# A two-layer encoder on one core: the 64-row score products become 128-row products with a zero-padded q

## The chip, the core and the metric

The kernel runs on one core of a Trainium2 chip. A core has five engines that work side by side, each through its own list of instructions in order: TensorE (PE in the profile; its weight loads are shown apart as PEld), VectorE (DVE), ScalarE (ACT), GpSimd (POOL) and SyncE (SP), which here issues all the DMA transfers. They wait for each other by semaphores. The metric is the device time of one execution in microseconds (us); less is better.

## What is computed

The reference is an encoder with 512 tokens of width 1024 and two layers. Each layer has a token mixer, a cross-attention into 256 memory tokens and a feed-forward part, each between two norms with a residual. Layer 1's mixer is dilated attention with 16 heads of 64 (layer "a"), layer 2's is differential attention with 8 pairs of heads of 64 (layer "b"). All in float32.

```python
def reference(x, mem, positions, ...):
    h = x
    for i in range(DEPTH):
        u = rms_norm(h, mix_pre_g[i])
        if kind == 0:
            y = dilated_attention_mixer(u, a_w_in[j], a_w_out[j], cos, sin)
        elif kind == 1:
            y = differential_attention_mixer(u, b_w_in[j], b_w_out[j], ..., cos, sin, i)
        ...
        h = h + rms_norm(y, mix_post_g[i])
        u = rms_norm(h, mem_pre_g[i])
        y = memory_cross_attention(u, rms_norm(mem, mem_kv_g[i]), x_wq[i], x_wkv[i], x_wo[i])
        h = h + rms_norm(y, mem_post_g[i])
        u = rms_norm(h, ffn_pre_g[i])
        y = swiglu_ffn(u, w_gate_up[i], w_down[i])
        h = h + rms_norm(y, ffn_post_g[i])
    return h
```

Both mixers need, for each head, scores q·k over 64 features for 512 queries by 512 keys, with q and k turned by a rotary embedding first.

## The kernel before

**Precision.** Every float32 operand of a matrix product is split into a high part (type fp32r in the profile) and a low part (what the high part left over). A product is then three products of parts: high·high, high·low and low·high. The splits cost one pass of ScalarE (high) and one of VectorE or GpSimd (low). For weights these are lines 237 and 238, after a DMA of 512 KB into one of two staging buffers `raw` (line 221).

**Scores.** A head has 64 features, so two of the three products fit into one: the stack `st[e]` of q holds q's high part of head e in 64 rows and its low part in the other 64, and k's stack holds k's high part twice. Line 645 multiplies the two over 128 rows, which gives high·high + low·high. Line 646 adds q high · k low over the 64 rows `a` of that head; k's low part `kl` holds both heads of a pair, one above the other. Each such pair of products fills one bank of PSUM (128 queries x 512 keys). A mixer has 8 pairs of heads (p = 0..7), each with 2 heads (e) and 4 blocks of 128 queries (qb): 64 score pairs in each layer, 128 in all.

**Making the stacks.** After the product that gives q of a pair, `q_stack` (line 577) applies the rotary embedding (`rope`: lines 560 and 561 on VectorE, 562 and 563 on GpSimd), makes the high part on ScalarE (line 592) and the low part on VectorE (line 594). Since the low part of a head belongs in the other 64 rows, `half_copies` (line 570) moves the four halves by DMA on SP's queue (line 573), 128 KB each. `k_stack` (line 600) does the same for k. Pair 7 (`DIRECT`) is written by the engines straight into the stacks (lines 586 and 587), without copies. The stacks of pairs p and p+2 share their memory.

**Order.** Two streams are written side by side by `drive`: the dense products of the mixer (`mixer`, `v_quarter`, `feat`: lines 312 to 314 and 626 to 628) and the attention (`attention`: scores, softmax, transposes of line 284, products with V of lines 719 and 742 to 744). A scheduler then sets the order of every engine from a model of times of its own; PE goes through its list in order, and so does SP. A score pair waits for its stacks, and for a free bank out of three.

Of the kernel before, what the change touches and what calls it, by code (L numbers as in the profile page):

```python
# [49 lines left out]
class Trunk:  # L50
    def __init__(self, tc, t, stack):
        self.tc = tc
        self.t = t
        pool = stack.enter_context(tc.tile_pool(name="sb", bufs=1))
        psum = stack.enter_context(
            tc.tile_pool(name="ps", bufs=1, space=bass.MemoryType.PSUM)
        )

        def sb(name, shape, dt=F32):
            return pool.tile(shape, dt, name=name)  # L60

        self.h = [sb(f"h{b}", [P, D]) for b in range(NB)]
        self.uh = sb("uh", [P, DK, S], F32R)
        self.ul = sb("ul", [P, DK, S], F32R)
        self.pool = pool
        self.R = [pool.tile([P, 2, S], F32R, name=f"r{i}", tag=f"r{i}") for i in range(22)]
        self.raw = [sb(f"raw{i}", [P, D]) for i in range(2)]
        self.wh = [sb(f"wh{i}", [P, D], F32R) for i in range(3)]
        self.wl = [sb(f"wl{i}", [P, D], F32R) for i in range(3)]
        self.g = [sb(f"g{i}", [P, D]) for i in range(2)]  # L70
        self.f = [sb(f"f{i}", [P, S]) for i in range(10)]
        self.junk = sb("junk", [P, D], BF16)
        self.ident = sb("ident", [P, P])
        self.mask = sb("mask", [P, 896])
        self.rc = sb("rc", [P, S])
        self.rs = sb("rs", [P, S])
        self.small = sb("small", [P, 160])
        self.half = sb("mhalf", [P, 1])
        self.lam = sb("lam", [P, 1])
        self.gsub = sb("gsub", [P, 1])  # L80
        self.bank = [psum.tile([P, S], F32, name=f"bank{i}") for i in range(8)]
# [18 lines left out]
        self.accs = self.bank[0:3]  # L100
        self.sbanks = self.bank[4:6]

# [1 line left out]
    def pick(self, what, items):  # L104
        i = self.rot.get(what, 0)
        self.rot[what] = i + 1
# [15 lines left out]
    def tbank(self):  # L122
        return self.pick("t", self.tbanks)

# [1 line left out]
    def pin(self, on):  # L126
        """Inside, the tensor engine keeps the order of emission."""
        if self.planning:
            return
        if on and self.pinned is None:  # L130
            self.pinned = self.tc.manual_schedule(engines={mybir.EngineType.PE})
            self.pinned.__enter__()
        if not on and self.pinned is not None:
            self.pinned.__exit__(None, None, None)
            self.pinned = None
# [15 lines left out]
            d[2]()  # L151

    def drive(self, dense, att=None, rate=1.0):
        """Emit two streams side by side; each yields a cost, or a condition to wait for."""
        streams = [dense, att] if att is not None else [dense]
        need = [None] * len(streams)
        done = [0.0] * len(streams)
        live = [True] * len(streams)
        base = [None]
        stuck = 0  # L160

        def free(i):
            return live[i] and (need[i] is None or need[i]())

        def step(i):
            try:
                if i == 1 and self.PRIO and not self.planning:
                    with self.tc.high_priority(offset=self.PRIO):
                        x = next(streams[i])
                else:  # L170
                    x = next(streams[i])
            except StopIteration:
                live[i] = False
                return
            if callable(x):
                need[i] = x
                return
            need[i] = None
            if i == 1 and base[0] is None:
                base[0] = done[0]  # L180
            done[i] += x
            self.tick(x)

        while any(live):
            if len(streams) == 2 and free(1):
                if not free(0) or base[0] is None or done[1] <= (done[0] - base[0]) * rate:
                    step(1)
                    continue
            if free(0):
                step(0)  # L190
            elif len(streams) == 2 and live[1] and need[1] is not None and not live[0]:
                need[1] = None
            else:
                stuck += 1
                assert stuck < 100, "stuck"
                self.tick(0.5)

# [1 line left out]
    def split(self, src, hi, lo):  # L199
        self.nc.scalar.activation(hi, src, AF.Copy)  # L200
        self.nc.vector.tensor_sub(lo, src, hi.bitcast(F32))
# [4 lines left out]
        return [self.R[i].rearrange("p a b -> p (a b)") for i in name]  # L206

    def plain(self, i):
        """The memory of R[i] as a float32 tile, until restore(i)."""
        return None if self.planning else self.pool.tile([P, D], F32, name=f"m{i}", tag=f"r{i}")  # L210

    def restore(self, i):
# [27 lines left out]
            )  # L240

    def weight(self, src, spare=None, gate=None, eng=0):
        """Next weight chunk as (hi, lo); spare names two R tiles, free once gate holds."""
        i = self.taken
        self.taken += 1
        if self.planning:
            if spare is None:
                spare = self.nring % 3
                self.nring += 1
            self.plan.append((src, eng, spare, gate))  # L250
        self.issue()
        assert self.planning or i < self.issued
        return (*self.buffers(self.plan[i][2]), i)
# [49 lines left out]
            )  # L303

    def feat(self, out, wh, wl, xh, xl, cols):
        """out [128 features, cols] += W^T x over 8 k-tiles; W tile is [P, 8, 128]."""
        nc = self.nc
        wh = wh.rearrange("p (k n) -> p k n", k=DK)
        wl = wl.rearrange("p (k n) -> p k n", k=DK)
# [11 lines left out]
        return self.ul[:, k]  # L321

    def feats(self, items, halves=0, eng=0, guards=None):
        """Feature-major products of u with weight tiles; items are (src, evac)."""
        full = slice(0, S)
        if halves:
            ws = [self.weight(src, eng=eng) for src, _ in items[:halves]]
# [17 lines left out]
            self.used(i)  # L345
            evac(bank)

# [1 line left out]
    def close(self, w, ktiles, act, ready, gpost, gnext, spares, between=None):  # L349
        """h += rms(act @ w) * gpost, then the next normalised transposed u."""  # L350
        nc = self.nc
        yg = self.f[0:4]
        m0 = [None] * NB
# [88 lines left out]
        if gnext is not None:  # L442
            self.norm_block(b, gnext(), 5.5)

# [1 line left out]
    def setup(self):  # L446
        nc, t = self.nc, self.t
        def x(b):
# [1 line left out]

        self.extra = [self.plain(i) for i in (4, 5, 6)]
        nc.vector.memset(self.half, -0.5)
        x(0)
        g = None
        for w in self.FIRST:
# [95 lines left out]
        nc.vector.tensor_scalar(self.lam, d, LAM_INIT, None, ALU.subtract)  # L551
        nc.vector.tensor_scalar(self.gsub, self.gsub, 1.0 - LAM_INIT, None, ALU.mult)

# [1 line left out]
    SWAP = [(i ^ 8) if i < 16 else i for i in range(32)]  # L555

    def rope(self, bank):
# [9 lines left out]
        return self.R[16 + 2 * (p % 2)], self.R[17 + 2 * (p % 2)], self.R[20][:, p % 2]  # L567

    def half_copies(self, src, st, swap):
        """Rows of head e of src into half e (or, swapped, the other half) of st[e]."""  # L570
        for e in (0, 1):
            a, o = slice(64 * e, 64 * e + 64), slice(64 - 64 * e, 128 - 64 * e)
            self.nc.sync.dma_start(
# [1 line left out]
            )  # L575

    def q_stack(self, p, bank):
        """st[0] = [hi0; lo0], st[1] = [lo1; hi1], scaled by 1/8."""
        nc = self.nc
        st = self.stacks(p)[0]  # L580
        hi, lo = self.R[21][:, 0], self.R[21][:, 1]
        x = self.rope(bank)
        if p in self.DIRECT:
            for e in (0, 1):
                a, o = slice(64 * e, 64 * e + 64), slice(64 - 64 * e, 128 - 64 * e)
                nc.scalar.activation(st[a, e], x[a], AF.Copy, scale=0.125)
                nc.vector.scalar_tensor_tensor(
                    st[o, e], x[a], 0.125, st[a, e].bitcast(F32), ALU.mult, ALU.subtract
                )
# [1 line left out]
            return  # L591
        nc.scalar.activation(hi, x, AF.Copy, scale=0.125)
        self.half_copies(hi, st, False)
        nc.vector.scalar_tensor_tensor(
            lo, x, 0.125, hi.bitcast(F32), ALU.mult, ALU.subtract
        )
# [1 line left out]
        self.mark["q", p] = self.clock  # L598

    def k_stack(self, p, bank):  # L600
        """st[e] = [hi_e; hi_e]; kl holds lo of both heads."""
        nc = self.nc
        _, st, kl = self.stacks(p)
        hi = self.R[21][:, 0]
# [8 lines left out]
        return self.R[8 + 2 * (j % 2) : 10 + 2 * (j % 2)]  # L613

    def v_quarter(self, j, src, hd, eng=0):
        """V of 256 columns, token-major: R tiles [P, 2 kb, 256/hd, (hi, lo), hd]."""
        nc = self.nc
        banks = [self.accbank() for _ in range(2)]
        ws = [self.weight(src[kc], eng=eng) for kc in range(2)]
# [20 lines left out]
    def scores(self, bank, p, e, qb):  # L640
        nc = self.nc
        qs, ks, kl = self.stacks(p)
        ts = slice(qb * P, (qb + 1) * P)
        a = slice(64 * e, 64 * e + 64)
        nc.tensor.matmul(bank, qs[:, e, ts], ks[:, e], start=True, stop=False)  # L645
        nc.tensor.matmul(bank, qs[a, e, ts], kl[a], start=False, stop=True)  # L646

    def p_views(self, pt, qb):
        o = slice((qb % 2) * P, (qb % 2) * P + P)
# [118 lines left out]
            self.later(1.5, rest)  # L768

    def attention(self, kind):  # L770
        """Softmax steps, each followed some steps later by its transposes and products."""
        queue = []
        npt = 0
        steps = []
# [82 lines left out]
    NORM_A = "vpva"  # L857
    NORM_B = "aaap"

# [1 line left out]
    def mem_load(self, i):  # L861
        nc = self.nc
        g = self.gain(1, self.t["mem_kv_g"][i : i + 1])
# [179 lines left out]

    XORDER = "k2 q1 k3 q2 q3"

# [1 line left out]
    def a_slot(self, k):  # L1047
        return self.R[16 + k] if k < 6 else self.R[2 + k] if k < 14 else self.R[k - 14]

# [223 lines left out]
```

## Time and profile before

| what | value |
|---|---|
| three runs, median (lowest, highest) | 1673.49 us (1672.62, 1676.25) |
| span of the profiled execution, first to last instruction | 1672.4 us |
| instructions in the span | 22109 |
| granted TensorE clock, mean | 0.998 |
| DMA moved, mean rate | 168.82 MB, 101 GB/s |

The time of the profiled execution beside its span is not given apart from the runs; the median of the runs is 1.1 us above the span.

How to read the profile's lines: a line of a group or of the timeline names the engine, the source line (L646 is line 646 of the kernel), the operation, what it writes and reads by the program's names (without buffer numbers, so `r` stands for all of the 22 large buffers and `bank` for the eight PSUM banks), the size of its tile in partitions x elements and a count. In the timeline the first number is the start in us from the start of the span and the second the duration; the bracket at the end is the idle time of that engine before the instruction and what ended it ("issue" when the profile shows nothing that it waited for). Products on PE are pipelined, so one lasts longer than the step from its start to the next one's: steps tell the throughput. In a list of waits a line gives the sum in us, how often, and the longest.

### The profile page before, as it was taken

Reading aid. Unit: us, or ns where it says so; the run is one execution under the profiler, and the core shown is the slowest. Engines: PE = TensorE matmul, PEld = TensorE weight load, DVE = VectorE, ACT = ScalarE, POOL = GpSimd, SP = SyncE. Lnnn points to the kernel's source line nnn. Section 1 sums busy time; section 2 is a strip of 40 time slices with the busy share of each in tenths; the row PEclk is TensorE's granted clock in tenths of the full one; section 3 lists DMA queues with packets and bytes.
Section 4 is the critical chain, followed back from the end, with each engine's and each line's share of the span. In section 5 each row is a group of like instructions: output and inputs, shape, how many; then the busy total and the mean of one; then the engine's idle time right before and its main releaser. Section 6 shows DMA issues by size and latency. Waiting matters only on the chain.

```text
span 1672.4 us, 22109 instructions
## 1 busy us (share of the span) xinstructions
PE 1640.3 (98%) x8696; PEld 1373.8 (82%) x8696; DVE 899.3 (54%) x1414; ACT 699.2 (42%) x1207; POOL 274.8 (16%) x264
## 2 busy tenths in 40 slices
PE   6999999999999999999999999999999999999998
PEld 6788788899888888888897787788988988888886
DVE  7668777654553333322367887856555433333223
ACT  4556666543443232222235655645344332232121
POOL 3543431100010000000044563411000000000000
PEclk9999999999999999999999999999999999999999
DMA  5413323343313223223423333243332223223222
GB/s 214 126 54 99 101 64 113 101 139 101 106 50 113 93 96 101 97 92 101 139 89 113 96 83 101 76 139 102 114 101 89 66 99 101 93 96 101 94 95 88
DMA packets 52616, 168.82 MB, mean 101 GB/s; under 512 B 7072, under 2 KB 7328, under 8 KB 52512
## 3 DMA queue, kind: packets, MB, share of 16 engines
q1 hardware_dynamic: 52512, 167.41, 31.4%
q8 instruction: 68, 1.11, 0.3%
q14 instruction: 36, 0.29, 0.1%
HBM read 148.51 MB, written 2.10 MB: 90 GB/s over the span
## 4 chain that ended last, share of the span: by engine, by line
PE 90%; DVE 4%; DMA 2%; ACT 1%; issue 1%; POOL 1%; SPq 0%; DVEq 0%; POOLq 0%; ACTq 0%
PE bank L313 15%; PE bank L312 15%; PE bank L314 15%; PE bank L364 7%; PE bank L366 7%; PE bank L365 7%; PE bank L284 4%; PE bank L646 3%; PE bank L627 2%; PE bank L626 2%; PE bank L628 2%; PE bank L645 2%; PE bank L719 2%; PE bank L913 1%; PE bank L915 1%
## 5 line engine op out<-in xcount | busy, mean ns | idle before, releaser
L237 ACT ACTIVATE wh<-raw 128x1024 fp32r<-128x1024 f32 x231 | 244.7, 1060 | 556.5 <-PE bank L313 232.6
L238 DVE TENSOR_TENSOR wl<-raw,wh 128x1024 fp32r<-128x1024 f32 x204 | 260.6, 1277 | 352.8 <-ACT wh L237 352.3
L312 PE MATMUL bank<-uh,wh 128*128 128x512 f32 (+1 forms) x1184 | 444.5, 376 | 0.5 <-ACT uh L288 0.5
L313 PE MATMUL bank<-ul,wh 128*128 128x512 f32 (+1 forms) x1184 | 444.1, 375 | 0.0
L314 PE MATMUL bank<-uh,wl 128*128 128x512 f32 (+1 forms) x1184 | 443.3, 375 | 0.0
L313 PEld LDWEIGHTS bank<-ul,wh 128*128 128x128 f32 x1184 | 224.0, 189 | 40.4 <-issue 3.3
L312 PEld LDWEIGHTS bank<-uh,wh 128*128 128x128 f32 x1184 | 223.8, 189 | 40.2 <-issue 2.2
L314 PEld LDWEIGHTS bank<-uh,wl 128*128 128x128 f32 x1184 | 224.0, 189 | 39.1 <-issue 2.2
L272 POOL TENSOR_SCALAR small<-small 128x1 f32<-128x1 f32 x76 | 24.6, 323 | 1109.1 <-ACT junk L265 1100.7
L364 PE MATMUL bank<-wh,r 128*128 128x512 f32 x400 | 156.5, 392 | 1.3 <-DVE f L755 0.8
L365 PE MATMUL bank<-wl,r 128*128 128x512 f32 x400 | 156.0, 390 | 0.0
L366 PE MATMUL bank<-wh,r 128*128 128x512 f32 x400 | 154.2, 390 | 0.0
L284 PE MATMUL bank<-ident,f 128*128 128x128 f32 x576 | 94.9, 278 | 16.5 <-DVE f L298 15.8
L1063 DVE TENSOR_TENSOR f<-f,bank 128x512 f32<-128x512 f32 x44 | 30.3, 688 | 142.9 <-PE bank L314 141.4
L284 PEld LDWEIGHTS bank<-ident,f 128*128 128x128 f32 x576 | 69.8, 142 | 29.4 <-DVE f L298 18.6
L364 PEld LDWEIGHTS bank<-wh,r 128*128 128x128 f32 x400 | 75.1, 188 | 18.5 <-DVE f L755 1.6
L365 PEld LDWEIGHTS bank<-wl,r 128*128 128x128 f32 x400 | 75.2, 188 | 14.7
L366 PEld LDWEIGHTS bank<-wh,r 128*128 128x128 f32 x400 | 74.8, 188 | 15.0
L288 ACT ACTIVATE r<-bank 128x512 fp32r<-128x512 f32 x104 | 60.9, 594 | 59.1 <-PE bank L284 56.9
L364 PE MATMUL bank<-r,r 128*128 128x512 f32 x208 | 82.8, 398 | 0.0
L365 PE MATMUL bank<-r,r 128*128 128x512 f32 x208 | 81.1, 390 | 0.0
L366 PE MATMUL bank<-r,r 128*128 128x512 f32 x208 | 79.6, 392 | 0.0
(170 smaller groups left out, 2764.9 us busy)
## 6 DMA issues: line engine op xcount, KB each, us to landing
raw<-in_gate_up SPq DMA_DIRECT2D x88, 512.0 KB, 3.2
raw<-in_down SPq DMA_DIRECT2D x44, 512.0 KB, 3.3
r<-r SPq DMA_DIRECT2D x120, 128.0 KB, 2.3
raw<-in_x_wk SPq DMA_DIRECT2D x16, 512.0 KB, 3.3
raw<-in_x_wv SPq DMA_DIRECT2D x16, 512.0 KB, 3.3
raw<-in_x_wq SPq DMA_DIRECT2D x16, 512.0 KB, 3.2
raw<-in_x_wo SPq DMA_DIRECT2D x16, 512.0 KB, 3.3
raw<-in_b_qk SPq DMA_DIRECT2D x16, 512.0 KB, 3.2
```

What stands on the lines that cost most here:

```text
L237: self.nc.scalar.activation(hi, raw, AF.Copy)
L238: (self.nc.gpsimd if eng else self.nc.vector).tensor_tensor(lo, raw, hi.bitcast(F32), ALU.subtract)
L284: nc.tensor.transpose(tb[:, k * P : (k + 1) * P], u[:, k * P : (k + 1) * P], self.ident)
L288: nc.scalar.activation(hi, tv, AF.Copy)
L312: nc.tensor.matmul(out, wh[:, k], xh(k)[:, cols], start=k == 0, stop=False)
L313: nc.tensor.matmul(out, wh[:, k], xl(k)[:, cols], start=False, stop=False)
L314: nc.tensor.matmul(out, wl[:, k], xh(k)[:, cols], start=False, stop=k == DK - 1)
L364: nc.tensor.matmul(out, ah[:, ts], hi[:, kk], start=k == 0, stop=False)
L365: nc.tensor.matmul(out, ah[:, ts], lo[:, kk], start=False, stop=False)
L366: nc.tensor.matmul(out, al[:, ts], hi[:, kk], start=False, stop=k == ktiles - 1)
L626: nc.tensor.matmul(out, uh, hi, start=k == 0, stop=False)
L646: nc.tensor.matmul(bank, qs[a, e, ts], kl[a], start=False, stop=True)
```

## The change

Two buffers `qz`, one for even and one for odd pairs, hold q's high part of head 0 in rows 0 to 63 of their first half and that of head 1 in rows 64 to 127 of their second half. The other rows are cleared once, at the start, by GpSimd. Line 646 (line 652 in the changed kernel) then multiplies all 128 rows of `qz` with all 128 rows of `kl`: the zeros take out the other head. `q_stack` fills `qz` with two more copies by DMA for each pair, between the copies of the high and of the low part, and for pair 7 with two more activations. To make room, the scratch for dynamic DMAs is set to 1024. The rest of the diff takes comments and docstrings out, which moves line numbers.

```diff
@@ __init__
         self.small = sb("small", [P, 160])
+        self.qz = [sb(f"qz{i}", [P, 2, S], F32R) for i in range(2)]
         self.half = sb("mhalf", [P, 1])
...
@@ setup
         nc.vector.memset(self.half, -0.5)
+        for z in self.qz:
+            nc.gpsimd.memset(z[64:128, 0].bitcast(F32), 0.0)
+            nc.gpsimd.memset(z[0:64, 1].bitcast(F32), 0.0)
         x(0)
...
@@ q_stack
         st = self.stacks(p)[0]
+        sz = self.qz[p % 2]
         hi, lo = self.R[21][:, 0], self.R[21][:, 1]
         x = self.rope(bank)
         if p in self.DIRECT:
             for e in (0, 1):
                 a, o = slice(64 * e, 64 * e + 64), slice(64 - 64 * e, 128 - 64 * e)
                 nc.scalar.activation(st[a, e], x[a], AF.Copy, scale=0.125)
+                nc.scalar.activation(sz[a, e], x[a], AF.Copy, scale=0.125)
                 nc.vector.scalar_tensor_tensor(
                     st[o, e], x[a], 0.125, st[a, e].bitcast(F32), ALU.mult, ALU.subtract
                 )
...
         nc.scalar.activation(hi, x, AF.Copy, scale=0.125)
         self.half_copies(hi, st, False)
+        self.half_copies(hi, sz, False)
         nc.vector.scalar_tensor_tensor(
...
@@ scores
         ts = slice(qb * P, (qb + 1) * P)
-        a = slice(64 * e, 64 * e + 64)
         nc.tensor.matmul(bank, qs[:, e, ts], ks[:, e], start=True, stop=False)
-        nc.tensor.matmul(bank, qs[a, e, ts], kl[a], start=False, stop=True)
+        nc.tensor.matmul(bank, self.qz[p % 2][:, e, ts], kl, start=False, stop=True)
...
@@ kernel
-    nc = bacc.Bacc("TRN2", target_bir_lowering=False, num_devices=1)
+    nc = bacc.Bacc(
+        "TRN2", target_bir_lowering=False, num_devices=1, dynamic_dma_scratch_size=1024
+    )
```

The scheduler's order moves with it. In the changed kernel line 645 is 651, 646 is 652, 573 is 577, 586 is 591 with 592 for the new activation, and lines 312 to 314 are 313 to 315. PE's list at the first three score pairs of layer 1, before (`bank_118` takes the product that gives k of pair 1, `r_84` and `r_83` are k's and q's stacks of pair 0, `r_87` is k's low part):

```order
L312 MATMUL bank_118<-uh,wh_93 128x512
L645 MATMUL bank_120<-r_84,r_83 128x512
L646 MATMUL bank_120<-r_87,r_83 128x512
L645 MATMUL bank_122<-r_84,r_83 128x512
L646 MATMUL bank_122<-r_87,r_83 128x512
L645 MATMUL bank_123<-r_84,r_83 128x512
L646 MATMUL bank_123<-r_87,r_83 128x512
L313 MATMUL bank_118<-ul,wh_93 128x512
```

The same place in PE's list now (`bank_120` takes the product for k; the first row is the same one as above):

```order
L313 MATMUL bank_120<-uh,wh_93 128x512
L314 MATMUL bank_120<-ul,wh_93 128x512
L315 MATMUL bank_120<-uh,wl_96 128x512
L313 MATMUL bank_120<-uh,wh_93 128x512
L651 MATMUL bank_122<-r_84,r_83 128x512
L652 MATMUL bank_122<-r_87,qz_115 128x512
L651 MATMUL bank_124<-r_84,r_83 128x512
L652 MATMUL bank_124<-r_87,qz_115 128x512
```

Three 512-column products of the dense stream have moved ahead of the first score, and the second product of a score reads `qz`. SP's list at the copies of k and q of pair 3 and of k of pair 4 in layer 1, before (`r_86` and `r_84` are k's stacks of odd and even pairs, `r_85` and `r_83` q's, `r_88` holds the parts before they are copied, `raw` rows are weight fetches):

```order
L573 DMA r_86<-r_88 64x512 x4
L221 DMA raw_89<-in_a_qk 128x1024
L573 DMA r_85<-r_88 64x512 x4
L221 DMA raw_90<-in_a_qk 128x1024
L573 DMA r_84<-r_88 64x512 x4
```

The same place in SP's list now:

```order
L577 DMA r_86<-r_88 64x512 x4
L222 DMA raw_89<-in_a_qk 128x1024
L577 DMA r_85<-r_88 64x512 x2
L577 DMA qz_116<-r_88 64x512 x2
L222 DMA raw_90<-in_a_qk 128x1024
L577 DMA r_85<-r_88 64x512 x2
L577 DMA r_84<-r_88 64x512 x4
```

The two new copies stand between those of the high part and those of the low part, and here a weight fetch has moved in ahead of the low part's; at the other q tiles of both layers the three groups stand together. ScalarE's list at pair 7 of layer 1, before (`f_105` is q after the rotary embedding, `r_85` its stack):

```order
L288 ACTIVATE r_79<-bank_125 128x4x128
L727 ACTIVATE f_107<-bank_121 64x512
L288 ACTIVATE r_81<-bank_124 128x4x128
L586 ACTIVATE r_85<-f_105 64x512 x2
L288 ACTIVATE r_75<-bank_125 128x4x128
```

The same place in ScalarE's list now:

```order
L289 ACTIVATE r_79<-bank_126 128x4x128
L677 ACTIVATE f_102,small<-f_102,small 128x512
L591 ACTIVATE r_85<-f_105 64x512
L592 ACTIVATE qz_116<-f_105 64x512
L591 ACTIVATE r_85<-f_105 64x512
L592 ACTIVATE qz_116<-f_105 64x512
L661 ACTIVATE f_102<-f_102,small 128x512
```

The two activations of the stack are now four, with the new ones in between.

## The prediction

> **What bounds the kernel now.** I read the page first: the busy time of each engine, then its chain of work that ended last.
>
> ```profile
> PE 1640.3 (98%) x8696; PEld 1373.8 (82%) x8696; DVE 899.3 (54%) x1414; ACT 699.2 (42%) x1207; POOL 274.8 (16%) x264
> PE 90%; DVE 4%; DMA 2%; ACT 1%; issue 1%; POOL 1%; SPq 0%; DVEq 0%; POOLq 0%; ACTq 0%
> ```
>
> TensorE (PE) is busy for 98% of the 1672.4 us span and carries 90% of the chain. Time taken out of its stream is time taken from the end, as long as the other engines keep up. Whether they can is a question for the two stages with scores, so I asked for the busy time by stage: the mixer of layer 1, the mixer of layer 2, and the stretch between them for comparison (columns: length, busy us and count for PE, PEld, DVE, ACT, POOL, then clock, DMA share, GB/s).
>
> ```profile
> 53.00:257.00 204.00, 200.78 (x1154) 161.43 (x1155) 158.47 (x347) 128.59 (x252) 81.59 (x52) 1.00 0.31 88
> 878.00:1074.00 196.00, 194.45 (x1030) 149.96 (x1031) 157.20 (x268) 114.27 (x229) 98.52 (x60) 0.99 0.34 97
> 320.00:845.00 525.00, 521.84 (x2636) 443.14 (x2635) 221.54 (x282) 179.41 (x279) 17.58 (x42) 1.00 0.30 100
> ```
>
> In the mixers VectorE (DVE) is busy 158.47 of 204 us (78%) and 157.20 of 196 us (80%); elsewhere it is at 42%. So PE bounds every stage, but with DVE not far behind in just the stages that the change touches. A busy PE is not a full PE, so next I looked at the starts in the timeline, in a quiet place of layer 2 (start, duration):
>
> ```profile
> 888.60 0.40 PE L313 MATMUL bank<-ul,wh 128*128 128x512 f32 x1
> 888.83 0.40 PE L645 MATMUL bank<-r,r 128*128 128x512 f32 x1
> 889.16 0.49 PE L646 MATMUL bank<-r,r 64*128 64x512 f32 x1
> 889.58 0.50 PE L314 MATMUL bank<-uh,wl 128*128 128x512 f32 x1
> 889.91 0.39 PE L312 MATMUL bank<-uh,wh 128*128 128x512 f32 x1
> ```
>
> Undisturbed 512-column products start 0.23 us apart (888.60 to 888.83). Around the 64-row one the steps are 0.33, 0.42 and 0.33: it starts late, its successor starts late, and the step after is still long. The three together take 1.08 us where three ordinary steps take 0.69: **0.39 us too much**. The weight loads say why:
>
> ```profile
> 52.17 0.39 PE L314 MATMUL bank<-uh,wl 128*128 128x512 f32 x1
> 52.17 0.19 PEld L312 LDWEIGHTS bank<-uh,wh 128*128 128x128 f32 x1
> 53.42 0.18 PEld L646 LDWEIGHTS bank<-r,r 64*128 64x128 f32 x1 [0.24 <-issue]
> 53.42 0.50 PE L646 MATMUL bank<-r,r 64*128 64x512 f32 x1
> 53.85 0.50 PE L645 MATMUL bank<-r,r 128*128 128x512 f32 x1
> 54.28 0.49 PE L646 MATMUL bank<-r,r 64*128 64x512 f32 x1
> ```
>
> An ordinary load starts together with the product before its own (52.17 and 52.17) and is done when its turn comes. The 64-row load starts only with its own product (53.42 and 53.42) after an idle 0.24 us. The array is emptied on the way into 64 rows and again on the way out.
>
> **The change: what it takes away.** Line 646 becomes a product over 128 rows, 64 of which are zero. Its form is then that of line 645 and of nearly everything around it, and such neighbours start 0.23 us apart. The price is the same where a 256-column product follows:
>
> ```profile
> 1092.02 0.39 PE L645 MATMUL bank<-r,r 128*128 128x512 f32 x1
> 1092.34 0.49 PE L646 MATMUL bank<-r,r 64*128 64x512 f32 x1
> 1092.76 0.39 PE L913 MATMUL bank<-wh,r 128*128 128x256 f32 x1
> 1092.98 0.28 PE L914 MATMUL bank<-wl,r 128*128 128x256 f32 x1
> 1093.10 0.28 PE L915 MATMUL bank<-wh,r 128*128 128x256 f32 x1
> ```
>
> From 1092.02 to 1092.98 are 0.96 us; without the change of form they would be 0.23 + 0.23 + 0.12 = 0.58 (0.12 being the step 1092.98 to 1093.10). That is 0.38 again. Where 64-row products alternate with line 645, one period is 54.28 − 53.42 = 0.86 us against 0.46, so 0.40. How many pay it? There are 128 score pairs (two layers, 64 each), but some 64-row products follow one another and share one switch:
>
> ```profile
> PEld bank L646 <- issue: 30.4, 108, 0.4
> 257.42 0.97 PE L646 MATMUL bank<-r,r 64*128 64x512 f32 x3
> ```
>
> 108 of the 128 loads show the idle time. 108 x 0.39 = **42.1 us**, about half in each layer. The two ends: adding up the starts around all 128 (the first at 53.42, the last at 1092.34), over what the same neighbours take elsewhere, gives 43.3 us; the idle of these loads alone is 30.4 us, which leaves out the long step behind them. I take 42.
>
> One rule of the Trainium skill speaks against it. "TensorE: Matmul & The Clock Gate", Part 3, says that a weight load overlaps running matmuls only when its row group differs from theirs; a 128-row load shares all rows with the 128-row product before it, so by that rule the wait would stay and the gain be nothing. The rows at 52.17 do not agree, since there a 128-row load runs beside a 128-row product. The rule is kept below as a rival.
>
> **What it adds.** (1) Two copies more for each of 14 q tiles (pair 7 of each layer takes another way), 28 in all, on SP's queue.
>
> ```profile
> L573 SPq DMA_DIRECT2D r<-r x120: 461/587/1637, 41.5 to 1064.0; - x120
> r<-r SPq DMA_DIRECT2D x120, 128.0 KB, 2.3
> 195.22 2.40 SPq L573 DMA_DIRECT2D r<-r  x4
> 199.74 0.84 PE L645 MATMUL bank<-r,r 128*128 128x512 f32 x3
> ```
>
> Each issue holds the queue 0.59 us, so q's low part is copied 1.2 us later, and whatever is queued behind, the weight fetches, too. Pair 5 of layer 1 shows how tight that is: the copies are issued until 197.6 and land 2.3 us later, at 199.9, and its first score stands at 199.74. If PE kept its old order, every such pair would stall by up to 1.2 us: 14 x 1.2 = 16.8 us at worst. But the order moves too: the first scores of layer 1 stand three 512-column products later (0.7 us), in the rows shown with the change. And no PE stall but these few stands in the two mixers (sum, times, longest):
>
> ```profile
> PE bank L284 <- DVE r L289: 2.2, 1, 2.2
> PE bank L645 <- DVE small L668: 1.0, 1, 1.0
> PE bank L913 <- ACT r L288: 0.7, 1, 0.7
> ```
>
> So between 0 and 16.8 us; I take 2, since most pairs are covered by the later place.
>
> (2) Pair 7 goes straight through ScalarE: two activations more for each layer.
>
> ```profile
> 255.05 1.28 ACT L586 ACTIVATE r<-f 64x512 fp32r<-64x512 f32 x2 [1.71 <-POOL f L563]
> 255.72 1.41 DVE L587 SCALAR_TENSOR_TENSOR r<-f,r 64x512 fp32r<-64x512 f32 x2
> 256.55 0.94 PE L645 MATMUL bank<-r,r 128*128 128x512 f32 x3
> ```
>
> One takes 0.64 us. The new one for the first head lies beside DVE's 0.70 us for that head, and the score waits for both anyway. The second head's stack comes 0.64 us later, and ACT's next work 1.28 us later. Between 0 and 1.28 us for each layer; I take 1 us for both together.
>
> (3) Four clears of 64x512 on POOL at the start, and a smaller scratch for DMAs.
>
> ```profile
> 5.45 0.19 POOL L272 TENSOR_SCALAR small<-small 128x1 f32<-128x1 f32 x1 [5.03 <-ACT junk L265]
> 0.93 0.48 DVE L516 MEMSET f<- 128x512 f32 x1
> 9.92 2.74 DVE L298 SCALAR_TENSOR_TENSOR f<-h,small,g 128x512 f32<-128x512 f32 x4 [7.97 <-DMA g<-in_mix_pre_g]
> ```
>
> POOL waits 5.03 us there. DVE clears twice that size in 0.48; even at twice that, four take 3.8. And the first step that needs POOL's result waits for a DMA until 9.92. Cost 0; without this cover it would be 3.8 at most. All DMA issues on the page are SP's, so a smaller scratch moves nothing.
>
> (4) Less slack. Each mixer loses about 21 us of PE time, and DVE's 157.2 us then fill 196 − 21 = 175 us to 90%, in layer 1 158.5 of 183, 87%. PE will now and then wait for a softmax. The fullest stretch the trace shows is 25.77 of 30 us, 86%:
>
> ```profile
> 20.00:50.00 30.00, 28.57 (x234) 28.16 (x234) 25.77 (x63) 11.36 (x18) 15.95 (x12) 1.00 0.36 117
> ```
>
> If 86% were the limit, layer 2 could not go below 157.2 / 0.86 = 183 us and layer 1 not below 184: a loss of 8 + 1 = 9 us. Between 0 and 9; I take 2, nearer to nothing, because the stages run at 78 and 80% today with under 3 us of PE waits each.
>
> (5) The clock.
>
> ```profile
> 880.00:884.60 4.60, 4.60 (x22) 4.11 (x22) 2.54 (x7) 3.05 (x7) 0.00 (x0) 0.63 0.49 114
> ```
>
> At the start of layer 2's scores the granted clock is 0.63 for 4.6 us, which costs 1.7 us. It may go or come once more: ±1.7, taken as 0.
>
> **Sum.** 1672.4 − 42.1 + 2 + 1 + 0 + 2 + 0 = 1635.3 us of span. The median of the runs, 1673.49, is 1.1 us above the profiled span, so on the scale of the runs **1636 us**.
>
> **The rivals.**
>
> *DVE and the copies take over.* The switch goes, but PE waits in its place: the 9 us of (4), half of the 16.8 of (1), and all 2.6 of (2) make 20 us, so 1673.5 − 42 + 20 = 1651; from 1643 up I count a result here. For it: DVE at 90%, and pair 5 that is covered today to 0.2 us. Against it: the small waits of today, and the later first scores.
>
> *Nothing happens.* The wait belongs not to the 64 rows but to the change of operand between 645 and 646, or the full-height load cannot be pulled ahead (the rule above). Then 128 pairs keep their 0.39 us and the copies cost 1 to 2: 1674 to 1676. Against it, the rows at 52.17, and that line 645 itself, of the same form, starts 0.23 us behind line 313.
>
> *Slower.* A weight fetch gets between q's high and low copies on SP's queue and blocks them.
>
> ```profile
> SPq L221 <- POOL wl L238: 93.0, 11, 15.8
> ```
>
> Such a fetch waits 93.0 / 11 = 8.5 us on average in layer 1. In the changed order one stands so, at pair 3. It could cost 8.5 us there; the kernel would get slower from five such places on (5 x 8.5 = 42.5 against 42), six giving 1673.5 − 42 + 51 = 1682. Against it: only one is seen.
>
> **How the numbers follow.** Forecast, a net loss of less than 12 us to what is added: 79%. DVE and copies: 15%. Nothing: 3%. Slower: 3%. The low end takes the 43.3 us, the clock stretch (1.7) and 2 to 3 us of today's stalls away: 1626. The high end goes to 1650, into the second case, and leaves out its upper part and the last two. About 0.2% (3.3 us) is what a measurement of this kernel can tell from no change: faster 94%, within it 3%, slower 3%.
>
> **What would show it.** In the new profile the start-to-start steps into and out of the second score product should be 0.23 us, and the row of idle before its load (30.4 us, 108 times) should be gone; PE's busy share stays near 98% and the two mixers are 17 to 21 us shorter each, the stretch between them unchanged at 525 us. Waits of line 645 for DMA or DVE that sum to over 10 us would show the first rival; steps still at 0.33 and 0.42 the second; SP waiting many us between an x2 of q's high part and its low part the third. I am wrong if the switch stays, or if the mixers shrink by less than 11 us each.

## The result

The changed kernel takes 1648.87 us (median of 4 runs, 1645.59 to 1650.55) against 1673.28 us: a ratio of 0.9846, 95% interval 0.9831 to 0.9861. That is 24.4 us or 1.5% less, and 13 us more than the forecast of 1636.

### The profile after

The page's busy line of the changed kernel and its chain of work, as they were shown of before:

```profile
PE 1607.1 (97%) x8696; PEld 1384.9 (84%) x8696; DVE 896.1 (54%) x1414; ACT 696.9 (42%) x1211; POOL 276.3 (17%) x268
PE 81%; DVE 8%; DMA 3%; POOL 3%; issue 3%; ACT 2%; SPq 0%; POOLq 0%; DVEq 0%; ACTq 0%
```

PE carries 81% of the chain, where it carried 90%, and DVE 8% instead of 4%. Other engines hold more of the chain than they did.

The steps are as forecast. From the timeline of the changed kernel (start, duration; 651 and 652 are the old 645 and 646):

```profile
66.97 0.39 PE L313 MATMUL bank<-uh,wh 128*128 128x512 f32 x1
67.19 0.40 PE L651 MATMUL bank<-r,r 128*128 128x512 f32 x1
67.42 0.40 PE L652 MATMUL bank<-r,qz 128*128 128x512 f32 x1
67.66 0.39 PE L314 MATMUL bank<-ul,wh 128*128 128x512 f32 x1
67.89 0.39 PE L315 MATMUL bank<-uh,wl 128*128 128x512 f32 x1
```

Each starts 0.23 us behind the one before it, where 0.33, 0.42 and 0.33 stood. The weight load of line 652 runs beside the 128-row product of line 651, and no row of line 652 is left in the list of the weight loads' waits:

```profile
67.19 0.19 PEld L652 LDWEIGHTS bank<-r,qz 128*128 128x128 f32 x1
```

The stages show where the time came from. From the busy time by stage, cut at the first and the last score of each layer, first before, then the changed kernel (columns as in the prediction):

```profile
53.00:269.90 216.90, 213.68 (x1234) 171.34 (x1234) 167.71 (x372) 136.80 (x269) 82.64 (x53) 1.00 0.30 86
269.90:878.10 608.20, 604.35 (x3165) 517.66 (x3165) 276.36 (x359) 218.35 (x344) 39.03 (x68) 1.00 0.32 103
878.10:1092.40 214.30, 212.25 (x1147) 164.30 (x1147) 171.81 (x295) 126.22 (x255) 99.99 (x61) 0.99 0.32 94
1092.40:1672.40 580.00, 570.57 (x2870) 483.04 (x2869) 246.96 (x313) 194.72 (x306) 27.72 (x57) 1.00 0.30 98
```

```profile
53.50:256.10 202.60, 195.60 (x1232) 175.01 (x1231) 168.48 (x372) 136.70 (x271) 81.88 (x53) 0.99 0.35 99
256.10:868.10 612.00, 607.15 (x3178) 520.44 (x3177) 275.90 (x360) 218.12 (x345) 38.80 (x68) 1.00 0.32 103
868.10:1064.20 196.10, 191.76 (x1144) 167.63 (x1145) 169.58 (x294) 124.56 (x255) 99.86 (x61) 0.98 0.38 109
1064.20:1648.70 584.50, 572.74 (x2859) 484.08 (x2857) 246.09 (x313) 194.25 (x307) 27.91 (x57) 0.99 0.29 98
```

The two stages with scores are 14.3 and 18.2 us shorter, which is 32.5 together, where 17 to 21 each were forecast. Outside them, where the edit changes no product, 3.8 and 4.5 us were lost, and the clock is no longer 1.00 in the last stage.

The list of PE's waits in the changed kernel's first stage and in its second:

```profile
PE bank L285 <- DVE r L290: 4.5, 2, 4.2
PE bank L651 <- DVE small L674: 1.8, 1, 1.8
...
```

```profile
PE bank L919 <- DVE f L565: 2.3, 1, 2.3
PE bank L651 <- DMA r<-r: 1.7, 2, 1.3
```

With the smaller rows they sum to 6.9 and 5.6 us, about twice what stood in the same stages before (3.4 and 2.5), and the largest sits at the end of a mixer, behind DVE. Waits for a copy are 1.7 us in all.

To account for the rest I added up, over all products of a profile, how much later each started than the ordinary step behind a product of its size (0.227 us for 512 columns, 0.119 for 256, 0.060 for 128), and put the excess down to the change of rows (steps next to a 64-row product), to stretches of half clock, or to waits (other steps over by 0.1 us). What is left is the stream of products itself. The experiments e1, e2 and e11 follow below.

| us | before | e1 (64 rows, all else as changed) | changed | e2 (qz not filled, order of before) | e11 (best) |
|---|---|---|---|---|---|
| start of the last product | 1665.7 | 1680.2 | 1642.0 | 1630.8 | 1631.3 |
| change of rows | 45.1 | 48.3 | 0 | 0 | 0 |
| waits of PE | 30.5 | 38.0 | 44.6 | 37.5 | 36.1 |
| half clock | 1.5 | 7.4 | 8.0 | 3.0 | 4.7 |
| the rest | 1588.6 | 1586.5 | 1589.4 | 1590.3 | 1590.5 |

The rest agrees within 4 us in five programs, so these three terms hold nearly all the difference: 45.1 us were gained, 14.1 us of waits and 6.5 us of half clock were given back. Each column is one execution. That of the changed kernel has the lowest clock of its four, so its 8.0 us of half clock are at the high end of what this program shows, and where a step is long in a stretch of half clock the division between these two rows is good to about 2 us.

**The clock.** At five places between the start and the last product the granted clock falls to half in the changed kernel, for 3.4 us each and once for 6.8, against one place before. Around two of them (busy by window of the changed kernel):

```profile
235.20:238.60 3.40, 0.08 (x2) 0.11 (x2) 3.40 (x6) 2.97 (x6) 0.89 (x1) 0.99 0.61 139
238.60:242.00 3.40, 3.40 (x16) 3.40 (x17) 2.77 (x6) 1.98 (x5) 0.00 (x0) 0.50 0.31 122
...
```

```profile
1109.00:1112.40 3.40, 1.42 (x8) 0.88 (x8) 1.21 (x3) 1.84 (x4) 1.83 (x4) 1.00 0.16 63
1112.40:1115.80 3.40, 3.40 (x14) 2.81 (x12) 2.85 (x6) 1.26 (x3) 0.03 (x1) 0.50 0.02 5
```

PE stands still for a good part of a window or all of it, and the next one runs at half clock. The four executions of the changed kernel go with this: spans of 1648.7 and 1648.8 us at a mean clock of 0.993, 1645.5 at 0.995, 1643.8 at 0.996. A mean of 0.993 is 11.5 us of full clock missing, 0.996 is 6.6 us; the difference, 4.9, is close to that of the spans, 5.0. (In the profiled one, at 0.993, some 2 us of this are a drop behind the last product, where PE has no more work.) It is no rule for every program: of e6's four executions the one at 0.997 took 1647.4 us and one at 0.996 took 1645.8.

### The profile page after: what moved, and what is told of

It is laid out like the page before. It is cut to its first block, busy times and chain, and to the rows that moved or that the text cites. A ratio compares the mean times of both kernels' runs of the same rounds, so it can differ in the third digit from the quotient of the medians.

```text
span 1648.7 us, 22174 instructions
## 1 busy us (share of the span) xinstructions
PE 1607.1 (97%) x8696; PEld 1384.9 (84%) x8696; DVE 896.1 (54%) x1414; ACT 696.9 (42%) x1211; POOL 276.3 (17%) x268
## 4 chain that ended last, share of the span: by engine, by line
PE 81%; DVE 8%; DMA 3%; POOL 3%; issue 3%; ACT 2%; SPq 0%; POOLq 0%; DVEq 0%; ACTq 0%
PE bank L314 14%; PE bank L313 14%; PE bank L315 14%; PE bank L365 7%; PE bank L367 7%; PE bank L366 7%; PE bank L285 4%; PE bank L725 2%; PE bank L651 1%; PE bank L652 1%; DVE wl L239 1%; PE bank L634 1%; PE bank L635 1%; PE bank L920 1%; PE bank L633 1%
## 5 line engine op out<-in xcount | busy, mean ns | idle before, releaser
L239 DVE TENSOR_TENSOR wl<-raw,wh 128x1024 fp32r<-128x1024 f32 x204 | 257.1, 1260 | 354.5 <-ACT wh L238 353.7
```

The source lines that it names most:

```text
L239: (self.nc.gpsimd if eng else self.nc.vector).tensor_tensor(lo, raw, hi.bitcast(F32), ALU.subtract)
```

## The experiments

The theory going in: the price is the change between 128 and 64 rows; what was missing from the gain is PE waiting for a DVE that is full at the ends of the mixers, and the clock that falls after such waits. Its rivals: the new copies themselves cost the time; the gain has another source than the rows. Times are medians of 4 runs, ratios are against before's runs beside them.

### e1: back to 64 rows, everything else as changed

```diff
-        nc.tensor.matmul(bank, self.qz[p % 2][:, e, ts], kl, start=False, stop=True)
+        a = slice(64 * e, 64 * e + 64)
+        nc.tensor.matmul(bank, self.qz[p % 2][a, e, ts], kl[a], start=False, stop=True)
```

> The changed kernel with one thing undone: the second score product reads the same new buffer qz and k's low part, but only the 64 rows of its head. All copies, clears and activations stay. Theory (the price is the change between 128 and 64 rows, about 0.39 us for each lone switch, 42 us in all): 1680 us or more, that is before's 1673 plus what the copies and the later order cost, with steps of 0.33 and 0.42 us around the second product and an idle of about 30 us before its loads. Rival (the gain comes from reading another buffer, or from the new order): close to the changed kernel's 1649.

1687.77 us, ratio 1.0084 (1.0069 to 1.0099). The order of the instructions on all five engines is the changed kernel's, so the two differ in the rows alone. The row of weight-load waits is back, in this kernel's list (line 653 is its second product):

```profile
PEld bank L653 <- issue: 31.5, 115, 0.4
```

With the rows the time goes from 1.0084 to 0.9846 of before's, 0.0238 or 40 us. This settles the price: 48.3 us of row changes in the table, 40 us net. It shows a second thing: with 64 rows the changed program is **14 us slower than before**. What was added around the product costs that much, and in the table above it is 7.5 us of waits and 5.9 of half clock. And a third: when the 48.3 us of row changes go, 6.6 us more of PE's waits come. Of the 14.1 us of waits given back, then, about half came with the additions and their order, and half with the lost slack.

### e2: qz never filled

```diff
-        self.half_copies(hi, sz, False)
...
-                nc.scalar.activation(sz[a, e], x[a], AF.Copy, scale=0.125)
```

with `qz` cleared whole at the start.

> The changed kernel without the 28 copies and 4 activations that fill qz; qz is cleared whole at the start, so the second product adds nothing (q high times k low is left out). Rows stay 128. Theory (what the change lost against the forecast is PE waiting for a full VectorE at the ends of the two mixers, and the clock that drops after such waits, not the copies): 1644 to 1651. Rival (the copies and activations delay the scores): 1630 to 1641, with the waits of line 651 for DMA and the long waits near 238 us and 1042 us of the changed kernel gone.

1639.47 us, ratio 0.9795 (0.978 to 0.981). The rival's range held, not mine: without the filling the kernel is 9 us faster. The profiled executions are 11 us apart, of which the table puts 7.1 to waits and 5.0 to the clock. But they aren't waits for copies, which are 1.7 us in all in the changed kernel.

The order of e2's instructions is that of before on every engine; only the second score product and the clears differ. So e2 against before is the switch alone in before's order: 34 us less, with 45.1 of row changes gone, 7.0 of waits and 1.5 of half clock added. It also shows that the filling moves the order and the rows don't, since e1, with 64 rows, has the changed kernel's order. The long wait at the end of the first mixer is, in this run's timeline, what it was before the change (2.17 us; line 290 copies the low part of a transposed tile out of its bank, and line 285 makes the next transposes):

```profile
236.47 0.68 DVE L290 TENSOR_TENSOR r<-bank,r 128x512 fp32r<-128x512 f32 x1
237.21 0.66 PE L285 MATMUL bank<-ident,g 128*128 128x128 f32 x4 [2.16 <-DVE r L290]
```

and in the changed kernel's timeline, at the same place in the program:

```profile
234.89 0.68 DVE L674 CUSTOM_DVE_ANT_0 f<-bank,mask 128x512 f32<-128x512 f32 x1
235.50 0.07 DVE L674 DVE_READ_ACCUMULATOR2_ANT small<- 128x1 f32 x1
235.50 1.67 DVE L239 TENSOR_TENSOR wl<-raw,wh 128x1024 fp32r<-128x1024 f32 x1
237.09 0.68 DVE L616 TENSOR_TENSOR r<-f,r 128x512 fp32r<-128x512 f32 x1
237.70 1.27 DVE L290 TENSOR_TENSOR r<-bank,r 128x512 fp32r<-128x512 f32 x2
238.52 0.41 PE L285 MATMUL bank<-ident,f 128*128 128x128 f32 x1 [4.19 <-DVE r L290]
```

DVE is never idle here. Its list has a softmax step, a weight split of 1.67 us and k's low part ahead of the copy out of the bank that PE waits for (line 290). In DVE's list of before, and of e2, these copies stand right behind the weight split, with no low part of k between them, and the softmax step stands well ahead of it. That the list was rearranged because the score stream starts later is my guess; no run shows it.

### e3: no activations for pair 7

```diff
                 nc.scalar.activation(st[a, e], x[a], AF.Copy, scale=0.125)
-                nc.scalar.activation(sz[a, e], x[a], AF.Copy, scale=0.125)
```

The second product of pair 7 then reads pair 5's q.

> The changed kernel without the 4 activations that fill qz for pair 7 of each mixer (the second product of that pair then reads pair 5's high part of q). The copies for pairs 0 to 6 stay. Theory (VectorE's list holds PE up near 238 us and 1042 us): within 3 us of 1649. Rival (two more activations on ScalarE hold up what stands behind them there): 1639 to 1645.

1646.32 us, ratio 0.9836 (0.9822 to 0.9851), which overlaps the changed kernel's interval. The wait at 238.5 us is still there, at 4.2 us. The four activations aren't its cause.

### e4: splits at the mixers' ends on GpSimd

```diff
-                ws.append(self.weight(w[0, c]))
+                ws.append(self.weight(w[0, c], eng=1))
...
-            hi, lo, i = self.weight(wk[2 * hd + c])
+            hi, lo, i = self.weight(wk[2 * hd + c], eng=int(hd == 0))
...
-        ws = [self.weight(wv[hd, kc]) for kc in range(2)]
+        ws = [self.weight(wv[hd, kc], eng=int(hd == 0)) for kc in range(2)]
```

> The changed kernel with the low-part split of the early chunks of the mixers' output weights and of the first cross-attention k and v weights moved from VectorE to GpSimd, all of which fall at the ends of the mixers. Theory (VectorE is full there): 3 to 10 us faster, 1639 to 1646, the 4.2 us wait near 238 us gone. Rival (GpSimd's slower split, 2.4 against 1.26 us, delays the rotary embedding of pair 7, which it also makes): no gain or slower, 1649 to 1656.

1643.9 us, ratio 0.9818 (0.9801 to 0.9834): 5 us under the changed kernel. The waits of its first stage read

```profile
PE bank L285 <- DVE r L290: 3.2, 3, 1.5
```

where 4.5 us stood, the longest 1.5 instead of 4.2. So DVE's list does hold PE there. (The order moved a little too, and the runs of e4 and of the changed kernel don't overlap, while their intervals just do.)

### e5 and e6: the same filling in other ways

e5 issues the copies into `qz` behind those of the low part:

```diff
-        self.half_copies(hi, sz, False)
...
         self.half_copies(lo, st, True)
+        self.half_copies(hi, sz, False)
```

> The changed kernel with the two copies into qz issued behind the copies of q's low part instead of ahead of them. Theory (any two more copies between q and its scores make the whole score stream start later, and it then ends with less dense work beside it): within 4 us of the changed kernel, 1645 to 1652. Rival (what costs is that the low part, which the first product needs, is copied 1.2 us later): 1638 to 1644, near the run without filling (1639.5).

1648.07 us, ratio 0.9836 (0.9821 to 0.9851): no difference from the changed kernel, as the theory had it. The delay of the low part isn't the price.

e6 fills `qz` by ScalarE instead of copies:

```diff
-        self.half_copies(hi, sz, False)
+        for e in (0, 1):
+            a = slice(64 * e, 64 * e + 64)
+            nc.scalar.activation(sz[a, e], x[a], AF.Copy, scale=0.125)
```

> The changed kernel with qz filled for all pairs by two ScalarE activations (0.62 us each) straight from the rotated q, as pair 7 has it, and no copies into qz. Theory (the 28 copies on SP's queue cost): 1637 to 1644, near the run without filling. Rival (any work more between q and its scores costs the same, on ScalarE too, which is at 60% in the mixers): 1646 to 1653.

1649.72 us, ratio 0.9844 (0.9828 to 0.9861). The rival held: 28 activations cost what 28 copies cost. SP's queue isn't it alone, then. What the variants share is more work between q and its scores, and an order that is not before's; each was measured in one order only.

### e7 and e8: padding k instead of q

Product 2 is q high times k low. With k's low part padded, q's whole stack can be multiplied with it; no copy is needed, and q's fills of `qz` are taken out as in e2.

```diff
-        nc.vector.tensor_sub(kl, x, hi.bitcast(F32))
+        for e in (0, 1):
+            a = slice(64 * e, 64 * e + 64)
+            nc.vector.tensor_sub(self.qz[p % 2][a, e], x[a], hi[a].bitcast(F32))
...
-        nc.tensor.matmul(bank, self.qz[p % 2][:, e, ts], kl, start=False, stop=True)
+        nc.tensor.matmul(bank, qs[:, e, ts], self.qz[p % 2][:, e], start=False, stop=True)
```

> The padding moved from q to k: two buffers hold k's low part of head 0 and of head 1 in its own 64 rows with zeros in the other 64, and the second product multiplies q's whole stack with it over 128 rows, which gives the same terms. No copy and no activation is added; VectorE writes the low part in two pieces of 64 rows instead of one of 128, 0.68 us more for each of 16 pairs. Theory (the copies cost 9 us of the gain): 1637 to 1644. Rival (VectorE is full in the mixers, so 11 us more of it cost as much): 1646 to 1655.

1650.05 us, ratio 0.9849 (0.9834 to 0.9864): no better than the changed kernel, though its 28 copies and 4 activations are gone. The rival's range held, by which 11 us more of DVE work (an estimate from 0.68 us for each of 16 pairs) cost as much; what of it is DVE's load and what the order was not separated. e8 puts the second piece (e = 1) on GpSimd:

> As the run before, with head 1's piece of k's low part on GpSimd instead of VectorE, so that VectorE has no more to do than in before. Theory: 1635 to 1643, and under the run before if VectorE's load counts. Rival (GpSimd, which also makes the rotary embedding, delays k): 1644 to 1652.

1644.78 us, ratio 0.9817 (0.9802 to 0.9831): 5 us better than e7, as if DVE's load counted, though the order moved as well. It misses the range that I gave (up to 1643) and lies in the rival's (from 1644), and is not at e2's 1639. The longest wait of its mixers is at another place, the end of the second mixer:

```profile
PE bank L285 <- DVE f L760: 4.3, 1, 4.3
```

### e9 to e12: putting them together, and the order alone

e9 is e8 with e4's splits.

> The padded k with head 1's piece on GpSimd (1644.8) together with the low-part splits at the ends of the mixers on GpSimd (which gave the changed kernel 5 us). Theory (the two take different work off: copies there, VectorE's list at the mixers' ends here): 1637 to 1642. Rival (GpSimd now has both and delays the rotary embedding of pair 7): 1644 to 1650.

1645.57 us, ratio 0.9831 (0.9814 to 0.9849): the rival, no gain over e8.

e10 changes the order alone:

```diff
-    RATE = (1.0, 1.0, 0.4)
+    RATE = (1.25, 1.25, 0.4)
```

> The changed kernel with the attention stream written out 25% faster against the dense stream in both mixers (rate 1.25 instead of 1), which changes the order alone. Theory (the later first scores leave the attention behind, so that it ends with less dense work beside it): 1639 to 1645, with the stage of scores shorter and the waits at the mixers' ends smaller. Rival (the order is set by the scheduler's own times, or the waits come from the copies themselves): 1646 to 1652.

1643.84 us, ratio 0.9819 (0.9803 to 0.9834). The same work in another order is worth 5 us, in the theory's range (the runs don't overlap with those of the changed kernel; the intervals just do). e11 has this rate and e4's splits.

> The changed kernel with both the splits at the mixers' ends on GpSimd and the rate of 1.25 (5 us each alone). If they take away different waits: 1637 to 1641. If both take away the same waits at the mixers' ends, or the order falls another way: 1642 to 1648.

**1639.27 us**, ratio 0.9786 (0.977 to 0.9802): the two add up, and this is the fastest kernel of the study, 9.6 us under the changed one, with all of the computation in it. Its waits in the table are 36.1 us against 44.6. e12 has the rate and e8's padded k.

> The padded k with head 1's piece on GpSimd, and the rate of 1.25. If the rate helps by the earlier attention stream: 1638 to 1642. If each order has its own waits and none is better by rule: 1643 to 1649.

1648.26 us, ratio 0.984 (0.9826 to 0.9855): 3.5 us slower than e8, with intervals that overlap. The rate isn't better by rule. Each order has its own few waits; where the order alone was changed (e10, and e12 against e8) the time moved by 5 and 3.5 us. How much of this lies in the scheduler's order and how much in what the added work takes at run time was not separated: no kernel had the additions with the order of before, and none the changed order without them.

## Why the prediction came out as it did

The time lies inside the range (1626 to 1650), near its upper end. By the prediction's own border, 1643, it belongs to the first rival, which had 15%, not to the forecast case, which had 79%. The gross gain was forecast well and what is given back was not: 5 us were forecast and about 20 came. The time is inside the range because its upper end reached into that rival's case. The rival's own sign, waits of line 645 for DMA or DVE above 10 us, did not show: line 651 waits 3.5 us for them, and the larger waits are at lines 285 and 919.

- **The switch, −42.1 us:** right in kind and in size. e1 gives 40 us net at an unchanged order, e2 34 us net at before's; the count over all starts gives 45 to 48. The rule of the Trainium skill that was kept as a rival is out: 128-row loads run beside 128-row products here (both start at 67.19), and the waits at line 652 are gone.
- **The copies, +2 us:** the step that failed first. The prediction bounded them by the time that a copy holds SP's queue, and took little of it because the first scores stand later in the new order. Waits for copies are indeed only 1.7 us. But the later place was counted as cover, and nothing was put for the rest of the new order: the lists of all engines are rearranged with the filling, and the ends of the mixers have longer waits behind DVE. e1 against before puts the additions at 14 us, of which 7.5 are waits and 5.9 half clock; e5 and e6 show no difference by how the filling is done. Whether the price is the order's or the work's stays open.
- **Pair 7, +1 us:** e3 measured 2.6 us, with overlapping intervals; not told apart from nothing.
- **The clears, 0:** right. The four take 0.52 us each and are done at 2.9 us.
- **Less slack, +2 us:** mis-sized. e1 against the changed kernel shows 6.6 us more of PE's waits at the same order, e2 against before 7.0 at the other. The limit that the prediction drew from the fullest stretch (9 us) was the closer number. It went "nearer to nothing" by the waits of before, which were counted while the long steps at the 64-row products were still hiding others; and in layer 1 they were 3.4 us, not under 3.
- **The clock, ±1.7, taken as 0:** the second step that failed. The row with 0.63 was read as one accident that might go or come. In the changed kernel each of the five drops follows a window in which PE stood still for 1.6 us or more, so more waits brought more of it: 6.5 us in the profiled execution, less in the two faster ones by their mean clock.
- **Not slower, not nothing:** right. The weight fetch between the copies of pair 3 (at 128.9 us) left no wait of PE behind it: the next one, of line 651 at 198 us (1.8 us), is for DVE.
- **What would show it:** the steps were right; the mixers shrank by 14.3 and 18.2 us where 17 to 21 was said, and the stretch between them was not unchanged.

In one line: 42 − 5 was forecast and 45 − 14 − 6.5 came.

## What to carry to other kernels

Look at start-to-start steps, not at busy time, for products with fewer rows among full ones: here each lone 64-row product cost 0.39 us beyond its own 0.23, which neither its duration nor PE's 98% shows. Padding such an operand with zeros removes it, but here the padding's own work, with the order that came with it, took 9 to 14 us back, however the buffer was filled. It pays to try a few orders of the same work: they differed by 3.5 and 5 us here, and by 10 with some splits moved to GpSimd. When a stage that was just bound by PE gets faster, count the waits that its slowness was hiding (7 us here), and expect some waits of about 2 us to be paid a second time through the clock.

## What was not expected of the hardware

The clock falls after waits well short of its own stretch. The Trainium skill, "TensorE: Matmul & The Clock Gate", Part 1, names a free-running window of 3413 ns and says that the clock goes to half after an idle one; the trace agrees in the lengths, with stretches of 3.41 and 6.83 us at 0.50, but the windows ahead of them were not idle throughout. The same page, section "Why this matters for your kernels", advises against idle gaps above about 3 us; here a single wait of 1.87 us was followed by such a stretch. From the timeline of the changed kernel, and its windows:

```profile
824.47 0.66 PE L285 MATMUL bank<-ident,f 128*128 128x128 f32 x4 [1.87 <-DVE f L299]
```

```profile
822.20:825.60 3.40, 1.53 (x9) 1.02 (x8) 1.95 (x3) 1.63 (x5) 1.87 (x4) 1.00 0.00 0
825.60:829.00 3.40, 3.40 (x11) 2.82 (x10) 2.60 (x5) 1.79 (x4) 0.46 (x2) 0.51 0.02 5
```

A wait of 2.17 us before the change, near 254 us, was not followed by one, while e2's wait of 2.16 us at the same place in the program was. What decides stays open: neither PE's busy time in a window nor that of its weight loads separates the two kinds here. Before's window at 877.7 us, with PE busy 2.98 of 3.40 us and its loads 1.55, was followed by a stretch at 0.50, and e8's at 1033.9 us, with 1.90 and 0.88, was not.
